# A two-layer hybrid backbone on one core: where the modulation bias is added

## The chip, the cores and the metric

The kernel runs on one core of a Trainium2 chip. Its time is the device time of one execution in microseconds (us), as the median of several runs. A trace of one execution shows every instruction of the five engines (PE is TensorE, with PEld its weight loads; DVE is VectorE; ACT is ScalarE; POOL is GpSimd; SP issues most of the loads) and the DMA queues.

## The reference

Two layers (weights differ per layer) run over 256 latent tokens and 256 context tokens of width 1024. All is float32. Before its mixers and before its FFN, each layer normalises the tokens and modulates them with a shift and a scale; each of the two residual branches is multiplied by a gate. These six vectors per layer come from one matrix-vector product with a bias, once for the latents (input `c`) and once for the context (input `c_ctx`):

```
s_c, s_cc = silu(c), silu(c_ctx)
m_l = split(s_c  @ w_mod[l] + b_mod[l], 6)     # latents: shift, scale, gate, shift, scale, gate
m_c = split(s_cc @ w_mod[l] + b_mod[l], 6)     # context
p   = (rms_norm(x) * (1 + m[1]) + m[0]) @ w_in[l]
x   = x + m[2] * merge(S5(p), retention(p), GLA(p), gates(p)) @ w_out[l]
x   = x + m[5] * swiglu(rms_norm(x) * (1 + m[4]) + m[3])
```

`w_mod[l]` is 1024 x 6144 and `b_mod[l]` 6144 long. The rest is three token mixers (a complex diagonal scan, retention, gated linear attention), three merge projections, an output projection and an FFN of width 2816. The change touches only how `+ b_mod[l]` is done.

## The kernel before, in words

**Weights.** Large products are made of three float32r products: each weight tile of 512 KB is loaded by SP into one of 3 `raw` buffers, split into a high part on ACT (line 264) and a low part on DVE (line 265) into one of 4 `hi`/`lo` pairs, and multiplied on PE (lines 243, 247 to 249). Weight loads and splits are traced with a priority 20000 instructions ahead of their place (`W_AHEAD`).

**The modulation vectors.** `self.sil` holds silu of both inputs, 128 rows by 8 blocks by 32 columns, of which two columns are in use (context, latent). The product of a vector is cut into four quarters of 256 columns. Quarter q is a product of 128 rows by 32 columns, written to partitions 32q to 32q+31 of one PSUM bank; rows 32q and 32q+1 are the context's and the latents' result.

- `mod_vec(l, m, gds)` (lines 340 to 396) makes ten of the twelve vectors, one at a time, beside the layers' own work: a list of "asides" is advanced by one step wherever the main code calls `tick()` (line 419). It loads a row of `b_mod` (line 347), begins the PSUM accumulation with four products of one row (`self.one`, all ones, times a quarter of the bias row; lines 348 to 350), loads eight blocks of `w_mod` of 512 KB into the two `wm` buffers (line 357), and adds their products. For the six vectors in `ON_VECTOR` the eight blocks are instead multiplied and summed on DVE (lines 362 to 367) and brought into PSUM at the end by products with `self.unit` (lines 369 to 372). Then ACT copies the bank into `rows` (line 376). Gates go to DRAM by four small stores (line 380); shifts and scales are transposed on PE and spread over `self.mod` by DVE (lines 383 to 395).
- `mod_chunk(c, brow)` (lines 431 to 459) makes the first two vectors of layer 0 in four chunks of 256 columns each at the start of the kernel. Both bias rows lie in the two `wm` buffers until the last chunk has used them (lines 1324 to 1327). Each chunk starts with four one-row products of 128 columns (line 445); ACT copies the result (line 451), PE transposes it, DVE spreads it (lines 455 to 458), `norm_chunk` modulates the tokens with it, and `pack_mms` multiplies them with the first weights.

**Order.** Each engine and each DMA queue works its instructions in order. The order is made by a planner that runs the program through its own timing model: an engine that is free takes the ready instruction of highest priority; an instruction whose buffer is not free is not ready. Tiles of the two arenas (`arena`, `zone`) are places chosen by the program, and a write waits for the last use of its place. SP's queue holds nearly all the loads, ACT's the token loads at the start, POOL's the small parameters.

Of the kernel before, what the change touches and what calls it, by code (L numbers as in the profile page):

```python
# [10 lines left out]
F32 = mybir.dt.float32  # L11
F32R = mybir.dt.float32r
U8 = mybir.dt.uint8
AF = mybir.ActivationFunctionType
ALU = mybir.AluOpType
# [4 lines left out]
D = 1024  # L20
KD = 8
# [118 lines left out]
class Hybrid:  # L140
# [199 lines left out]
    def mod_vec(self, l, m, gds):  # L340
        nc, i = self.nc, self.i
        b = self.bank(self.sd)[:, :256]
        ring = lambda: self.wmod.tile([128, D], F32, tag="wm", name=self.nm("wm"))
        c0 = D * m
        with self.prio(-W_AHEAD - self.delta):
            brow = self.new(D)
            self.q["mod"].dma_start(out=brow.ap[0:1], in_=i["b_mod"][l:l + 1, c0:c0 + D])
        for q in range(4):
            self.mm_(b[32 * q:32 * q + 32], self.one[0:1], brow.ap[0:1, 256 * q:256 * q + 256], True, False,
                     tile_position=(0, 32 * q))  # L350
        dve = (l, m) in ON_VECTOR
        who = (1,) if l and m > 1 else (0, 1)
        acc = {x: self.new(D) for x in who} if dve else {}
        for k in range(KD):
            with self.prio(-W_AHEAD - self.delta):
                w = ring()
                self.q["mod"].dma_start(out=w, in_=i["w_mod"][l, 128 * k:128 * k + 128, c0:c0 + D])
            if not dve:
                for q in range(4):
                    self.mm_(b[32 * q:32 * q + 32], self.sil[:, k], w[:, 256 * q:256 * q + 256], False, k == KD - 1,  # L360
                             tile_position=(0, 32 * q))
            for x, a in acc.items():
                c = self.sil[:, k, x:x + 1]
                if k:
                    self.stt(a.ap, w, c, a.ap, ALU.mult, ALU.add)
                else:
                    self.ts(a.ap, w, c, None, ALU.mult)
            yield
        for x, a in acc.items():
            for q in range(4):  # L370
                self.mm_(b[32 * q:32 * q + 32], self.unit[:, x], a.ap[:, 256 * q:256 * q + 256], False, x == 1,
                         tile_position=(0, 32 * q))
            self.drop(a)
        self.drop(brow)
        rows = self.new(256)
        self.act(rows.ap, b, AF.Copy)
        if m in (2, 5):
            gd = gds[m]
            for q in range(4):
                self.q["gd"].dma_start(out=gd[:, 256 * q:256 * q + 256], in_=rows.ap[32 * q:32 * q + 2])  # L380
            self.drop(rows)
            return
        tb = self.bank(self.sd)
        for k in range(2):
            self.transpose(tb[:, 128 * k:128 * k + 128], rows.ap[:, 128 * k:128 * k + 128])
        tv = tb[:, :256].rearrange("p (k q s) -> p q k s", q=4, s=32)[:, :, :, 0:2]
        idx = {0: 0, 1: 1, 3: 2, 4: 3}[m]
        dst = self.mod[:, l, idx].rearrange("p (q k) s -> p q k s", k=2)
        if m in (1, 4):
            g0 = 32 * l + (0 if m == 1 else 8)  # L390
            for s in range(2):
                self.stt(dst[:, :, :, s], tv[:, :, :, s], 1.0,
                         self.par[:, g0:g0 + 8].rearrange("p (q k) -> p q k", k=2), ALU.add, ALU.mult)
        else:
            nc.vector.tensor_copy(dst, tv)
        self.drop(rows)
# [34 lines left out]
    def mod_chunk(self, c, brow):  # L431
        nc, i = self.nc, self.i
        b = self.bank()
        ws = {}
        for m in (1, 0):
            ws[m] = (self.zone if c == 3 and m else self.arena).new(KD, 256)
            self.q["modc"].dma_start(out=ws[m].ap, in_=i["w_mod"][0][:, D * m + 256 * c:D * m + 256 * c + 256].rearrange(
                "(k p) c -> p k c", p=128))
        for k in range(KD + 1):
            for q in range(4):  # L440
                m, hf = q // 2, q % 2
                o = b[32 * q:32 * q + 32, :128]
                if k == 0:
                    c0 = 256 * c + 128 * hf
                    self.mm_(o, self.one[0:1], brow[m][0:1, c0:c0 + 128], True, False, tile_position=(0, 32 * q))
                else:
                    self.mm_(o, self.sil[:, k - 1], ws[m].ap[:, k - 1, 128 * hf:128 * hf + 128], False, k == KD,
                             tile_position=(0, 32 * q))
        self.drop(*ws.values())
        rows = self.new(128)  # L450
        self.act(rows.ap, b[:, :128], AF.Copy)
        tb = self.bank()
        self.transpose(tb[:, :128], rows.ap)
        tv = tb[:, :128].rearrange("p (m k s) -> p m k s", m=2, s=32)
        for s in range(2):
            self.stt(self.mod[:, 0, 1, 2 * c:2 * c + 2, s], tv[:, 1, :, s], 1.0, self.par[:, 2 * c:2 * c + 2],
                     ALU.add, ALU.mult)
        nc.vector.tensor_copy(self.mod[:, 0, 0, 2 * c:2 * c + 2], tv[:, 0, :, 0:2])
        self.drop(rows)
# [855 lines left out]
    def layer(self, l):  # L1315
        nc = self.nc
# [4 lines left out]
        if l == 0:  # L1321
            with self.prio(-2 * W_AHEAD):
                self.load_params()
                brow = [self.wmod.tile([128, D], F32, tag="wm", name=self.nm("wm")) for _ in range(2)]
                xin = [self.x_in(t) for t in range(4)]
                for m in range(2):
                    self.q["par0"].dma_start(out=brow[m][0:1], in_=self.i["b_mod"][0:1, D * m:D * m + D])
                xs = [self.xscale(x.ap, self.arena if t > 1 else self.zone) for t, x in enumerate(xin)]
                hold = self.zone.new(1536)
                self.drop(*xin)  # L1330
                banks = [self.bank(self.mm) for _ in range(4)]
                for c in range(4):
                    self.mod_chunk(c, brow)
                    self.norm_chunk(c, xs)
                    self.pack_mms(banks, self.pack_weights(0, 0, c), c)
                self.drop(*xs)
            gqk = self.pack_out(0, banks, u_dr)
            self.load_params2()
        else:
            self.need("mod10")  # L1340
            gqk = self.pack_early(l, u_dr)
            self.drop(*self.xt[:2])
            x_dr = self.dram.tile([2, 128, D], F32, name=self.nm("xdr"))
            for t in range(2):
                self.q["xst"].dma_start(out=x_dr[t], in_=self.xt[2 + t].ap)
                self.drop(self.xt[2 + t])
# [107 lines left out]
```

## Time and profile before

| | |
|---|---|
| timed runs (3) | 1404.64, 1400.70, 1400.59 us; median 1400.7 |
| profiled execution, first to last instruction | span 1395.2 us (mean granted TensorE clock 0.985) |
| what lies around the span | 5.5 us, median less span |
| busy: PE / PEld / DVE / ACT / POOL | 1344.3 / 1140.9 / 908.3 / 577.4 / 75.6 us |
| instructions | 22070 |

The profiled execution's own device time is not given; its span and the 5.5 us around it are what the numbers below are added to. Busy time of an engine says little by itself; PE is busy 96% of the span, and where it is busy without a pause a product that goes can shorten the run. A chain of waits, followed back from the end, says which work set the end.

### The profile page before, as it was taken

The page shows a single profiled execution, that of the slowest core. Times are in us where ns is not written, and L with a number is a line of the kernel's source. Part 1 is how long each engine was busy: PE and PEld are TensorE (multiplying, and loading weights), DVE is VectorE, ACT ScalarE, POOL GpSimd, SP SyncE. Part 2 cuts the span into 40 slices and gives each one's busy share as a digit, 9 for nine tenths or more (in the row PEclk, how much of TensorE's full clock was granted, in tenths as well). Part 3 has the DMA queues.
Part 4 walks back from the last instruction along what each step waited for, and adds up shares of the span by engine and source line. Part 5 has one row for each costly group of instructions (what it writes and reads, how often), then busy time and mean ns, then how long its engine had stood idle before and what let it go on. Part 6 is the DMA issues. An engine that isn't in the chain of part 4 may idle for free.

```text
span 1395.2 us, 22070 instructions
## 1 busy us (share of the span) xinstructions
PE 1344.3 (96%) x8559; PEld 1140.9 (82%) x8559; DVE 908.3 (65%) x1423; ACT 577.4 (41%) x930; POOL 75.6 (5%) x111
## 2 busy tenths in 40 slices
PE   4899999999999999999999999999999999899996
PEld 3788888787777778788777778888999997899985
DVE  4579782838889564545554788645876778555555
ACT  3367352323432343222222447545564364444442
POOL 3310000001100020000000000100000100000000
PEclk9999999999999999999999999999999999899999
DMA  9744465668968554733344786644766866466662
GB/s 305 213 115 119 139 200 182 213 197 271 303 210 280 173 165 125 234 109 121 106 129 129 279 310 193 181 112 111 199 170 163 238 191 215 117 198 197 184 192 91
DMA packets 258817, 257.33 MB, mean 184 GB/s; under 512 B 27200, under 2 KB 219244, under 8 KB 258200
## 3 DMA queue, kind: packets, MB, share of 16 engines
q1 hardware_dynamic: 244360, 230.41, 55.0%
q10 hardware_dynamic: 11392, 20.39, 4.2%
q0 software_dynamic: 2960, 5.12, 1.4%
q8 instruction: 67, 1.10, 0.3%
q14 instruction: 38, 0.31, 0.1%
HBM read 231.79 MB, written 24.08 MB: 183 GB/s over the span
## 4 chain that ended last, share of the span: by engine, by line
PE 85%; DMA 6%; DVE 5%; issue 2%; ACT 2%; SPq 1%; DVEq 0%; POOL 0%; POOLq 0%; ACTq 0%
PE b L243 83%; PE b L253 2%; DVE arena L231 2%; DVE lo L231 1%; DMA wm<-in_w_mod_dram 1%; DMA arena<-in_w_mod_dram 1%; DMA raw<-in_w_in_dram 1%; DMA raw<-in_w_ffn_out_dram 1%; DMA arena<-wb 1%; ACT arena L228 1%; DMA arena<-in_ctx_dram 1%; ACT hi L228 1%; DVE rb L231 0%; DVE zone L234 0%; DMA raw<-in_w_ffn_in_dram 0%
## 5 line engine op out<-in xcount | busy, mean ns | idle before, releaser
L243 PE MATMUL b<-rb,hi 128*128 128x256 f32 (+1 forms) x2784 | 695.1, 340 | 6.2 <-ACT rb L228 4.7
L243 PEld LDWEIGHTS b<-rb,hi 128*128 128x128 f32 x2784 | 481.9, 193 | 70.1 <-issue 11.1
L228 ACT ACTIVATE hi<-raw 128x1024 fp32r<-128x1024 f32 (+3 forms) x298 | 293.0, 989 | 458.0 <-PE b L243 350.4
L243 PE MATMUL b<-rb,lo 128*128 128x256 f32 (+1 forms) x1392 | 471.3, 339 | 0.0
L231 DVE TENSOR_TENSOR lo<-raw,hi 128x1024 fp32r<-128x1024 f32 (+3 forms) x298 | 338.3, 1140 | 199.4 <-ACT hi L228 190.4
L243 PE MATMUL b<-hi,rb 128*128 128x512 f32 (+2 forms) x1168 | 346.2, 374 | 3.9 <-DVE arena L570 3.3
L243 PEld LDWEIGHTS b<-rb,lo 128*128 128x128 f32 x1392 | 268.7, 193 | 31.7 <-issue 5.4
L243 PEld LDWEIGHTS b<-hi,rb 128*128 128x128 f32 x1168 | 216.5, 188 | 39.2 <-issue 4.1
L243 PE MATMUL b<-lo,rb 128*128 128x512 f32 (+2 forms) x584 | 217.0, 373 | 0.0
L243 PE MATMUL b<-arena 64*64 64x96 f32 (+8 forms) x1104 | 132.8, 288 | 0.3 <-DVE arena L231 0.3
L243 PEld LDWEIGHTS b<-lo,rb 128*128 128x128 f32 x584 | 109.8, 188 | 15.3 <-issue 1.3
L243 PEld LDWEIGHTS b<-arena 128*128 128x128 f32 (+4 forms) x1104 | 102.6, 167 | 20.2 <-issue 7.1
L231 DVE TENSOR_TENSOR arena<-arena 128x512 f32<-128x512 f32 (+5 forms) x174 | 105.6, 622 | 17.7 <-ACT arena L228 16.7
L234 DVE SCALAR_TENSOR_TENSOR arena<-arena,b 128x512 f32<-128x512 f32 (+1 forms) x136 | 74.2, 552 | 51.0 <-PE b L243 50.6
L228 ACT ACTIVATE arena<-b 128x512 f32<-128x512 f32 (+6 forms) x138 | 66.5, 486 | 73.9 <-PE b L243 59.6
L228 ACT ACTIVATE rb<-arena 128x256 fp32r<-128x256 f32 (+3 forms) x133 | 60.8, 473 | 84.3 <-PE b L243 57.2
L231 DVE TENSOR_TENSOR zone<-zone 128x512 f32<-128x512 f32 (+6 forms) x127 | 73.7, 604 | 28.6 <-DMA wb<-zone 17.4
L234 DVE SCALAR_TENSOR_TENSOR zone<-wm,sil,zone 128x1024 f32<-128x1024 f32 x56 | 70.9, 1283 | 18.7 <-DMA wm<-in_w_mod_dram 18.3
L231 DVE TENSOR_TENSOR rb<-arena,rb 128x256 fp32r<-128x256 f32 (+2 forms) x106 | 54.4, 522 | 21.1 <-ACT rb L228 20.7
L228 ACT ACTIVATE arena<-arena 128x512 f32<-128x512 f32 (+3 forms) x61 | 36.5, 601 | 30.6 <-DVE arena L231 19.9
L253 PE MATMUL b<-cst,arena 128*128 128x128 f32 (+1 forms) x178 | 30.4, 290 | 18.8 <-DMA arena<-in_norm_mix_dram 9.6
L491 POOL TENSOR_TENSOR st<-st,mh 128x1 f32<-128x1 f32 x16 | 11.6, 727 | 658.9 <-DVE st L240 657.9
(137 smaller groups left out, 660.4 us busy)
## 6 DMA issues: line engine op xcount, KB each, us to landing
raw<-in_w_ffn_in_dram SPq DMA_DIRECT2D x88, 512.0 KB
wm<-in_w_mod_dram SPq DMA_DIRECT2D x80, 512.0 KB
raw<-in_w_ffn_out_dram SPq DMA_DIRECT2D x66, 512.0 KB
raw<-in_w_in_dram SPq DMA_DIRECT2D x48, 512.0 KB
raw<-in_w_in_dram SPq DMA_DIRECT2D x48, 384.0 KB
raw<-in_w_out_dram SPq DMA_DIRECT2D x16, 512.0 KB
arena<-in_w_mod_dram SPq DMA_DIRECT2D x7, 1024.0 KB
wb<-zone ACTq DMA_DIRECT2D x8, 512.0 KB
```

The costliest lines, as they stand in the source:

```text
L228: self.S.activation(out, in_, f, bias=bias, scale=scale)
L231: self.V.tensor_tensor(out=out, in0=a, in1=b, op=op)
L234: self.V.scalar_tensor_tensor(out=out, in0=a, scalar=s, in1=b, op0=op0, op1=op1)
L243: self.P.matmul(out, l, r, start=start, stop=stop, **k)
L253: self.P.transpose(out, in_, self.ident[:k, :k])
L491: self.G.tensor_tensor(out=st[:, 3:4], in0=st[:, 2:3], in1=self.mh[:, 0:1], op=ALU.pow)
```

## The change

The one-row products go. The bias is loaded to the partitions where the result lies (32q and 32q+1, both rows the same), over a buffer that POOL has set to zero, and DVE adds it while it copies the result out of PSUM, where ACT copied it before. The first product of each accumulation now opens it. In `mod_vec` the bias buffer is 256 columns instead of 1024 and becomes the result; its one load becomes four. At the start the two `wm` buffers with bias rows become one, zeroed by POOL, and the two loads become four.

```diff
@@ mod_vec
         with self.prio(-W_AHEAD - self.delta):
-            brow = self.new(D)
-            self.q["mod"].dma_start(out=brow.ap[0:1], in_=i["b_mod"][l:l + 1, c0:c0 + D])
-        for q in range(4):
-            self.mm_(b[32 * q:32 * q + 32], self.one[0:1], brow.ap[0:1, 256 * q:256 * q + 256], True, False,
-                     tile_position=(0, 32 * q))
+            brow = self.new(256)
+            nc.gpsimd.memset(brow.ap, 0.0)
+            for q in range(4):
+                self.q["mod"].dma_start(out=brow.ap[32 * q:32 * q + 2],
+                                        in_=i["b_mod"][l, c0 + 256 * q:c0 + 256 * q + 256].partition_broadcast(2))
...
-                    self.mm_(b[32 * q:32 * q + 32], self.sil[:, k], w[:, 256 * q:256 * q + 256], False, k == KD - 1,
+                    self.mm_(b[32 * q:32 * q + 32], self.sil[:, k], w[:, 256 * q:256 * q + 256], k == 0, k == KD - 1,
...
-                self.mm_(b[32 * q:32 * q + 32], self.unit[:, x], a.ap[:, 256 * q:256 * q + 256], False, x == 1,
+                self.mm_(b[32 * q:32 * q + 32], self.unit[:, x], a.ap[:, 256 * q:256 * q + 256], x == who[0], x == 1,
...
-        self.drop(brow)
-        rows = self.new(256)
-        self.act(rows.ap, b, AF.Copy)
+        rows = brow
+        self.tt(rows.ap, b, brow.ap, ALU.add)
@@ mod_chunk
-        for k in range(KD + 1):
+        for k in range(KD):
...
-                if k == 0:
-                    c0 = 256 * c + 128 * hf
-                    self.mm_(o, self.one[0:1], brow[m][0:1, c0:c0 + 128], True, False, tile_position=(0, 32 * q))
-                else:
-                    self.mm_(o, self.sil[:, k - 1], ws[m].ap[:, k - 1, 128 * hf:128 * hf + 128], False, k == KD,
-                             tile_position=(0, 32 * q))
+                self.mm_(b[32 * q:32 * q + 32, :128], self.sil[:, k], ws[m].ap[:, k, 128 * hf:128 * hf + 128], k == 0,
+                         k == KD - 1, tile_position=(0, 32 * q))
...
-        self.act(rows.ap, b[:, :128], AF.Copy)
+        self.tt(rows.ap, b[:, :128], brow[:, c], ALU.add)
@@ layer, at the start of layer 0
-                brow = [self.wmod.tile([128, D], F32, tag="wm", name=self.nm("wm")) for _ in range(2)]
+                brow = self.wmod.tile([128, D], F32, tag="wm", name=self.nm("wm"))[:, :512]
+                nc.gpsimd.memset(brow, 0.0)
+                brow = brow.rearrange("p (c j) -> p c j", j=128)
                 xin = [self.x_in(t) for t in range(4)]
-                for m in range(2):
-                    self.q["par0"].dma_start(out=brow[m][0:1], in_=self.i["b_mod"][0:1, D * m:D * m + D])
+                for q in range(4):
+                    self.q["par0"].dma_start(out=brow[32 * q:32 * q + 2], in_=self.i["b_mod"][
+                        0, D * (q // 2):D * (q // 2) + D].rearrange("(c h j) -> h c j", h=2, j=128)[q % 2].partition_broadcast(2))
```

## Rows read from the trace of the kernel before

**Rows 1.** The page: busy time of each engine; the chain of waits by engine.

```profile
PE 1344.3 (96%) x8559; PEld 1140.9 (82%) x8559; DVE 908.3 (65%) x1423; ACT 577.4 (41%) x930; POOL 75.6 (5%) x111
PE 85%; DMA 6%; DVE 5%; issue 2%; ACT 2%; SPq 1%; DVEq 0%; POOL 0%; POOLq 0%; ACTq 0%
```

**Rows 2.** Stretches: length; PE, PEld, DVE, ACT, POOL busy; clock; DMA share; GB/s.

```profile
10.00:11.00 1.00, 0.05 (x1) 0.00 (x0) 0.36 (x3) 0.19 (x2) 0.31 (x1) 1.00 0.98 384
48.00:50.00 2.00, 1.64 (x61) 1.37 (x52) 2.00 (x4) 0.78 (x2) 1.51 (x3) 1.00 0.96 254
450.00:650.00 200.00, 199.99 (x1067) 160.15 (x1066) 105.80 (x149) 63.23 (x101) 8.51 (x12) 1.00 0.51 155
776.00:838.00 62.00, 61.68 (x305) 48.16 (x303) 50.40 (x62) 30.49 (x46) 0.00 (x0) 1.00 0.88 312
```

**Rows 3.** Groups of PE, shapes apart: the one-row products of `mod_vec`.

```profile
L243 PE MATMUL b<-zone,one 1*32 1x256 f32 x80 | 6.3, 386 | 1.3 <-DMA zone<-in_b_mod_dram 1.3
```

**Rows 4.** Timeline of PE, three places: start, time, line, operation, count, idle before.

```profile
244.55 0.63 PE L243 MATMUL b<-zone,one 1*32 1x256 f32 x8
245.12 1.07 PE L243 MATMUL b<-wm,sil 128*32 128x256 f32 x16
...
389.02 0.62 PE L243 MATMUL b<-rb,hi 128*128 128x512 f32 x2
389.48 0.39 PE L243 MATMUL b<-rb,lo 128*128 128x512 f32 x1
389.79 0.63 PE L243 MATMUL b<-zone,one 1*32 1x256 f32 x8
390.36 0.73 PE L243 MATMUL b<-rb,hi 128*128 128x512 f32 x2
390.93 0.39 PE L243 MATMUL b<-rb,lo 128*128 128x512 f32 x1
...
410.33 0.63 PE L243 MATMUL b<-zone,one 1*32 1x256 f32 x8 [1.34 <-DMA zone<-in_b_mod_dram]
```

**Rows 5.** The chain that ended last, in order of time, two stretches: start, time.

```profile
289.73 8.69 DMA arena<-wb
...
321.61 8.50 PE b L243 x57
...
754.58 21.85 PE b L243 x119
...
838.30 13.25 PE b L243 x57
```

**Rows 6.** Groups of DVE by shape: sums of two tensors that are near.

```profile
L231 DVE TENSOR_TENSOR arena<-b,arena 128x256 f32<-128x256 f32 x8 | 3.4, 422 | 0.4 <-PE b L243 0.3
L231 DVE TENSOR_TENSOR rb<-raw,rb 128x128 fp32r<-128x128 f32 x8 | 2.3, 291 | 4.4 <-ACT rb L228 4.3
```

**Rows 7.** Timeline of the first 48 us, three engines: PE, DVE, SP.

```profile
46.18 0.33 PE L253 MATMUL b<-cst,arena 128*128 128x128 f32 x1 [1.40 <-ACT arena L228]
...
45.69 1.29 DVE L231 TENSOR_TENSOR lo<-raw,hi 128x768 fp32r<-128x768 f32 x2 [6.76 <-ACT hi L228]
...
47.94 1.00 SPq L357 DMA_DIRECT2D wm<-in_w_mod_dram  x2
```

**Rows 8.** SP's waits up to 60 us: us in total, times, longest.

```profile
SPq L1327 <- DMA arena<-in_ctx_dram: 3.1, 1, 3.1
SPq L437 <- DMA arena<-in_ctx_dram: 2.2, 1, 2.2
```

**Rows 9.** Bias loads of `mod_vec` (min/median/max ns) and two in SP's timeline.

```profile
L347 SPq DMA_DIRECT2D zone<-in_b_mod_dram x10: 243/258/288, 222.1 to 800.5; - x10
222.12 5.09 SPq L347 DMA_DIRECT2D zone<-in_b_mod_dram x2
```

**Rows 10.** Timeline of POOL: a memset; a load that waited.

```profile
39.08 0.52 POOL L760 MEMSET arena<- 128x512 f32 x1 [0.98 <-PE b L243]
447.44 1.72 POOL L991 DMA_DIRECT2D zone<-in_s_b_re_dram  x2 [91.32 <-DMA gd<-zone]
```

More of the change, by code (lines that the diff above doesn't have):

```diff
@@ L438, in mod_chunk @@
                 "(k p) c -> p k c", p=128))
-        for k in range(KD + 1):
+        for k in range(KD):
             for q in range(4):
                 m, hf = q // 2, q % 2
-                o = b[32 * q:32 * q + 32, :128]
-                if k == 0:
-                    c0 = 256 * c + 128 * hf
-                    self.mm_(o, self.one[0:1], brow[m][0:1, c0:c0 + 128], True, False, tile_position=(0, 32 * q))
-                else:
-                    self.mm_(o, self.sil[:, k - 1], ws[m].ap[:, k - 1, 128 * hf:128 * hf + 128], False, k == KD,
-                             tile_position=(0, 32 * q))
+                self.mm_(b[32 * q:32 * q + 32, :128], self.sil[:, k], ws[m].ap[:, k, 128 * hf:128 * hf + 128], k == 0,
+                         k == KD - 1, tile_position=(0, 32 * q))
         self.drop(*ws.values())
         rows = self.new(128)
-        self.act(rows.ap, b[:, :128], AF.Copy)
+        self.tt(rows.ap, b[:, :128], brow[:, c], ALU.add)
         tb = self.bank()
```

## The prediction

> **What bounds the kernel now.** I read the page first: PE is busy 96% of the span and holds 85% of the chain that ended last; DVE is next with 65% [rows 1]. Then the stretches, since a share is a mean. From 450 to 650 us PE pauses for 0.01 us in 200: there a product that goes shortens the run by its slot. In 776:838 PE is as full, but DVE is busy 81% and the DMA engines 88% at 312 GB/s; in 48:50, at the start, DVE is busy all the time [rows 2]. Third the chain in order of time, to see which of two full engines sets the pace. It leaves PE twice in the range of the change: from 289.73 us (DRAM round trips and scans of the S5 mixer) until 321.61, and from 776.43 (754.58 + 21.85) until 838.30, where it runs through loads of `w_mod` and FFN weights, high parts on ACT, low parts and `mod_vec` sums on DVE [rows 5]. What PE saves inside these two stretches is slack; before and between them it counts.
>
> **The change part by part.**
>
> *One-row products of `mod_vec`: removed.* Ten vectors by four products are 40, seen as 80 records, 6.3 us busy, and PE waited 1.3 us for one bias row [rows 3]. What a site costs is read from starts [rows 4]. Where the vector's own products follow at once, 245.12 - 244.55 = 0.57 us; four sites do (244, 291, 445, 506 us). Where it stands alone between 512-column products, these run at (389.48 - 389.02) / 2 = 0.23 us; from 389.48 to 390.93 there are three of them and the site, so 1.45 - 0.69 = 0.76 us: the products around it lose 0.2 us as well. Six sites are so (338, 390, 410, 577, 784, 810 us); that at 410.33 has the wait of 1.34 us besides. In all 4 x 0.57 + 6 x 0.76 + 1.34 = 8.2 us leave PE's queue. Of these, the sites at 291 (0.57), 784 and 810 (2 x 0.76) lie in the two stretches where the chain is not PE's, and count nothing. That leaves 6.1 us. The wait at 410: PE has no other pause near it, so what comes late next can only be DVE, which I give nothing there; if it is as late, 1.3 us less.
>
> *The sum on DVE: added; ACT's copy: removed.* Ten DVE sums of 128x256 with one operand in PSUM. The same form elsewhere takes 0.422 us [rows 6]. Eight lie in stretches where PE sets the pace and DVE has over a third of its time free: nothing. The two of the last vectors (near 799 and 826 us) are in line on DVE where the chain runs through it: 2 x 0.42 = 0.84 us, with 0 below if their wait for a load hides them. ACT is idle enough that its copies give nothing back. Behind each sum wait the low parts queued on DVE, which PE needs only some tiles later (four `hi`/`lo` pairs).
>
> *Bias loads.* Four for one: 30 more issues on SP, 0.258 us each [rows 9], 7.7 us over 1400, hidden by the three `raw` buffers; in 776:838 at most one vector's three more, 0.8 us, which I leave to the range. They are needed only at the end of a vector, so their landing is hidden. POOL's ten memsets are half of a 128x512 one of 0.52 us [rows 10], on an engine busy 5%: nothing.
>
> *The start.* Four chunks lose four one-row products each. Those of the first two chunks ran while PE waited for `w_mod` anyway, those of the fourth between waits: nothing; the third's, in a full stretch of PE, half a 256-column site, 0.3 us. The result now passes DVE: a 128x128 sum is 0.29 us [rows 6]. For the first two chunks DVE is free. For the last two it lies in 44:54, where DVE is full: 2 x 0.29 = +0.6 us. Here is the widest unknown, the third chunk's order on DVE. Before, PE's transposes waited 1.40 us at 46.18 because ACT split a weight ahead of its copy; if DVE now takes the sum ahead of its low parts (45.69 to 46.98), that goes: -1.4. If behind them, the sum ends at 46.98 + 0.29 instead of before 46.18: +1.1 [rows 7]. Each is as likely; I take the 0.6 and 0.3 between. Next, one `wm` buffer is free from the start. Its first 512 KB were loaded at 47.94, as soon as the bias rows were used, though needed at 245 [rows 7, 4]: the planner takes a load when its buffer is free. It will now stand among the first loads, 512 KB at 384 GB/s [rows 2] or 1.4 us; it counts if it delays the fourth chunk's weights (which ended in the split at 45.69) and these are then what is waited for: 0 to +1.4, and I take 0.4, since the chunk's products are 10 us later. Last, SP: the first bias load and a `w_mod` load waited for the context tokens, which they don't use (3.1 and 2.2 us) [rows 8]; the eighth load before each is what fits, four of SP and four of ACT being ahead of the first. Two more bias loads push the first `w_mod` loads two turns back, behind the second context block and the first of `x`. The DMA engines are then full with those tokens (98% in 10:11, 384 GB/s) [rows 2], so little is lost: 0 to +2.8, and I take 0. Start in all: +0.6 - 0.3 + 0.4 = +0.7 us, between -1.7 (-1.4 - 0.3) and +5.6 (1.1 + 0.6 + 1.4 + 2.8 - 0.3).
>
> *Sum.* -6.1 + 0.8 + 0.7 = -4.6 us on a span of 1395.2; with the 5.5 us around it, the median of 1400.7 becomes 1396.1. With each unknown at its end, from 1400.7 - 8.2 - 1.7 = 1390.8 (all sites count, DVE's sums hidden, a good start) to 1400.7 - 6.1 + 1.3 + 0.8 + 0.8 + 5.6 = 1403.1.
>
> **The rivals.**
>
> *All of it counts.* The chain's leaving PE need not mean that PE has slack: at 838.30 PE paused little, and 61.68 of 62 us in 776:838 it was busy [rows 2]. If DVE is late there only because the planner lets it be, all 8.2 us count, DVE's sums cost nothing, and the third chunk gains 1.4 + 0.3: 1390.8. Against it: 88% DMA share there.
>
> *The start gives most of it back.* The extra `w_mod` load goes ahead of the fourth chunk's weights (+1.4), the sum of the third stands behind their low parts (+1.1), the first `w_mod` pair is 2.2 us late (the second's wait of before). With 0.6 for the full DVE and the 0.3 saved that is +5.0 against -6.1 + 0.8: 1400.4, no change. For it: the DMA engines are full at the start, 98% in 10:11 [rows 2]. Against: three things must meet.
>
> *Slower: the bias loads hold SP's queue.* One mechanism: a bias load waits for POOL's memset and for the eighth load before it, and all weight loads stand behind it. Its place is where the chain goes through loads: the start and 776:838. Two bias loads in a row once took 5.09 us [rows 9]; a vector now has four in a row. If each of the two vectors in 776:838 holds the queue for those 5.1 us, and the start loses 2.8, that is +13.0 against -6.1 + 0.8 + 0.7: 1409.1. It decides from where the hold is longer than the buffers cover; below 2.3 us a vector it stays a gain. For it: POOL's head once waited 91 us for a store [rows 10], and a memset behind such a head would hold SP too. Against: bias loads were issued far ahead of their use, all but one. The Trainium skill, "DMA: Bandwidth & Descriptors", section "Rules for kernel authors", speaks for it: "Many small transfers | Coalesce into one large transfer; under 64 KB you're paying mostly overhead". The change splits 4 KB in four. By the 2.0 us of fixed cost in its section "Anatomy of one DMA", fitted there to POOL's loads, 30 more are an estimated 60 us if none of it were hidden; the trace shows 0.26 us of SP each and one wait of PE.
>
> That the products would not go is no rival: nothing else of the kernel issues them.
>
> **How the numbers follow.** The sum above: 0.43. All of it counts: 0.20. The start gives it back: 0.24. SP's queue held: 0.13. The median is 1396.1, the likeliest's own range 1392 to 1400. The range for 8 in 10 goes from 1390 (the second case) to 1404 (past the third, into part of the fourth). A measurement of this kernel tells about 0.3%, 4.2 us: faster is below 1396.5, slower above 1404.9. Faster holds the second case and a little over half of the first with some of the third's better half: 0.49; no change the rest of the first and most of the third: 0.37; slower the fourth: 0.14.
>
> **What would show it.** In the trace after: no `one` products on PE, and 512-column products running on at 0.23 us where sites stood; at 410 no pause; ten DVE sums of 0.42 us reading PSUM and `zone`; PE full in 450:650. For the start: where the sum of the third chunk stands to the low parts at 45, when the first `w_mod` load is issued, and whether PE's pause of 1.40 at 46 us is gone. For the held queue: SP waiting at line 347's successors with weights late behind, and pauses of PE after 776. The prediction is wrong if PE's busy time falls by less than 6 us, or if it falls and the pauses grow by as much elsewhere than at the start.

## The result, and the profile after

The changed kernel takes 1418.3 us (median of 5 runs, 1412.4 to 1420.3) against 1400.7: the ratio is 1.0118, 95% interval 1.0096 to 1.0140. It is slower by 17.6 us, where 4.6 us less was forecast. Its page has these lines (span; busy time; the chain that ended last, by engine):

```profile
span 1416.3 us, 21921 instructions
PE 1347.5 (95%) x8447; PEld 1144.1 (81%) x8447; DVE 916.3 (65%) x1437; ACT 571.8 (40%) x916; POOL 78.9 (6%) x122
PE 78%; DMA 9%; issue 4%; DVE 4%; ACT 2%; SPq 2%; POOL 0%; ACTq 0%; DVEq 0%; POOLq 0%
```

PE has 112 products fewer (records of the trace) and is busy 3.2 us longer than in [rows 1]; PE's share of the chain fell from 85% to 78%. Stretches of the kernel before and of the changed one show where (length; PE, PEld, DVE, ACT, POOL busy; granted clock; DMA share; GB/s). First the kernel before:

```profile
0.00:110.00 110.00, 85.39 (x632) 70.71 (x633) 67.75 (x160) 48.23 (x83) 30.74 (x59) 0.98 0.69 205
110.00:440.00 330.00, 328.35 (x2159) 264.96 (x2158) 245.98 (x369) 128.76 (x200) 16.11 (x14) 0.99 0.68 209
440.00:900.00 460.00, 459.37 (x2419) 365.48 (x2418) 277.04 (x380) 165.88 (x264) 12.06 (x17) 1.00 0.56 178
900.00:1395.00 495.00, 471.24 (x3356) 439.74 (x3353) 317.55 (x517) 234.52 (x383) 16.72 (x21) 0.97 0.59 170
```

Then the changed kernel, with the two stretches that answer to [rows 2] at the end:

```profile
0.00:110.00 110.00, 81.86 (x577) 67.62 (x578) 67.27 (x165) 44.68 (x76) 32.15 (x62) 0.95 0.69 205
110.00:440.00 330.00, 319.82 (x2070) 256.86 (x2068) 237.44 (x355) 126.33 (x195) 24.77 (x30) 0.96 0.67 204
440.00:900.00 460.00, 456.75 (x2364) 366.41 (x2364) 282.49 (x385) 159.39 (x250) 5.61 (x9) 1.00 0.55 173
900.00:1416.00 516.00, 489.11 (x3441) 453.24 (x3439) 329.08 (x534) 241.43 (x398) 16.40 (x21) 0.97 0.59 170
...
450.00:650.00 200.00, 199.11 (x1048) 160.01 (x1047) 111.69 (x159) 60.95 (x95) 3.21 (x4) 1.00 0.51 160
776.00:838.00 62.00, 59.63 (x265) 47.33 (x264) 42.22 (x51) 23.46 (x34) 0.00 (x0) 0.97 0.76 253
```

The reader is to take two numbers from each: the pause (length less PE's busy time) and the loss to the clock (length times what is missing of 1.00). In 110:440 PE's pauses grew from 1.7 to 10.2 us and the loss to the clock from 1.7 to 13.7 (from stretches of 1 us; the rounded clocks above give 3.3 and 13.2). Over the whole span the pauses are 68.8 us instead of 50.9 (+17.9), and the loss to the clock is 35.4 instead of 20.9 (span times one less the mean clock of 0.975 and 0.985). Part of this loss lies in the pauses. Taken in slices of 1 us, the loss inside PE's busy time is 26.3 us instead of 15.0 (+11.3), and PE's work at the full clock is 1321.2 instead of 1329.3 (-8.1). The three differences sum to the +21.1 of the spans. So the work did leave PE, 8 us of it, and 29 us of pauses and half-speed came in its place. A second profile of the kernel before (c_before below) has 57.2, 11.7 and 1331.2 us: single profiles differ by some us.

**What came as foreseen.** No product with `one` is left. The ten sums on DVE take 0.42 us, the 40 bias loads 0.25 us of SP each, and no product waits for a bias load (groups of DVE; the loads with min/median/max ns):

```profile
L231 DVE TENSOR_TENSOR zone<-b,zone 128x256 f32<-128x256 f32 x10 | 4.2, 417 | 2.6 <-PE b L243 2.6
...
L349 SPq DMA_DIRECT2D zone<-in_b_mod_dram x40: 231/252/446, 218.0 to 754.7; - x40
```

**The start.** The timelines that answer to [rows 7], SP, PE and DVE (start, time, what, idle before):

```profile
5.09 3.24 SPq L1323 DMA_DIRECT2D wm<-in_b_mod_dram  x4
8.38 2.06 SPq L436 DMA_DIRECT2D arena<-in_w_mod_dram  x2
...
33.18 3.05 SPq L357 DMA_DIRECT2D wm<-in_w_mod_dram  x1
...
39.26 0.33 PE L253 MATMUL b<-cst,arena 128*128 128x128 f32 x1 [1.67 <-DVE arena L231]
43.53 0.30 PE L243 MATMUL b<-arena,sil 128*32 128x128 f32 x2 [2.14 <-DMA arena<-in_w_mod_dram]
57.17 0.33 PE L253 MATMUL b<-cst,arena 128*128 128x128 f32 x1 [0.41 <-DVE arena L231]
62.22 1.28 PE L243 MATMUL b<-rb,hi 128*128 128x512 f32 x4 [3.14 <-ACT rb L228]
...
56.83 0.29 DVE L231 TENSOR_TENSOR arena<-b,wm 128x128 f32<-128x128 f32 x1 [5.43 <-PE b L243]
```

The first `w_mod` pair is issued at 8.38 us, two turns later, and the first `wm` load at 33.18, as worked out. But the planner made another order of it: the third chunk comes sooner (its transposes at 39.26 instead of 46.18, behind a pause of 1.67 us where 1.40 stood), and the fourth's products run in four pieces among the third's, until 56.8 us, so that its row is summed at 56.83. Before, ACT copied it at 49.71:

```profile
49.71 0.28 ACT L228 ACTIVATE arena<-b 128x128 f32<-128x128 f32 x1 [1.21 <-PE b L243]
```

PE then pauses 3.14 us, and its clock is at half level (1.2 GHz) from 63.2 for 6.8 us.

**Near 420 us.** The chain in order of time (start, time, what):

```profile
396.08 4.29 DMA wm<-in_w_mod_dram
400.37 0.02 issue
400.40 1.02 DVE zone L238
401.42 0.03 issue
401.45 6.94 DMA wm<-in_w_mod_dram
...
409.80 4.88 DMA wm<-in_w_mod_dram
...
418.75 5.20 DMA wm<-in_w_mod_dram
...
425.25 1.30 DVE rb L231 x2
426.55 0.04 issue
426.59 5.67 PE b L243 x18
```

DVE works in order; the sums of a vector on DVE stand ahead of the low part that PE needs, and each waits for its 512 KB of `w_mod`, of which only two fit. PE pauses 9.29 us before 426.59, and its granted clock is 0.53 in 421:432. DVE's operations on `wm` show this wait over the kernel (us, times), first before, then the changed kernel:

```profile
  DMA wm<-in_w_mod_dram: 22.2, 17
...
  DMA wm<-in_w_mod_dram: 42.8, 29
```

Beside these loads POOL's of the second layer's S5 preparation run now, which waited until 447 us before [rows 10]:

```profile
399.55 0.31 POOL L347 MEMSET zone<- 128x256 f32 x1 [25.94 <-PE b L243]
400.07 1.77 POOL L985 DMA_DIRECT2D zone<-in_s_b_re_dram  x2 [0.20 <-issue]
```

**Where the loss is made.** Both kernels have 5928 products of a token block with a weight part. Counted by these (the n-th of one against the n-th of the other, where the two orders agree), the changed kernel is 7 us late where before stands at 65 us, 13 at 193, 12 at 403 and 20 at 420; from 450 us on it stays 18 to 23 us late. So the whole loss is made in the first 440 us.

### The profile page after: what moved, and what is told of

It reads as the page before. It is cut to its first block, busy times and chain, and to the rows that moved or that the text cites. A ratio compares the mean times of both kernels' runs of the same rounds, so it can differ in the third digit from the quotient of the medians.

```text
span 1416.3 us, 21921 instructions
## 1 busy us (share of the span) xinstructions
PE 1347.5 (95%) x8447; PEld 1144.1 (81%) x8447; DVE 916.3 (65%) x1437; ACT 571.8 (40%) x916; POOL 78.9 (6%) x122
## 4 chain that ended last, share of the span: by engine, by line
PE 78%; DMA 9%; issue 4%; DVE 4%; ACT 2%; SPq 2%; POOL 0%; ACTq 0%; DVEq 0%; POOLq 0%
PE b L243 77%; DMA wm<-in_w_mod_dram 5%; PE b L253 1%; DVE zone L234 1%; DMA arena<-in_w_mod_dram 1%; ACT arena L228 1%; DVE lo L231 1%; SPq L436 1%; DVE arena L231 1%; DMA arena<-in_x_dram 1%; ACT hi L228 1%; SPq L534 0%; DMA udr<-arena 0%; DMA arena<-gdr 0%; DMA zone<-in_s_log_dt_dram 0%
## 5 line engine op out<-in xcount | busy, mean ns | idle before, releaser
L243 PEld LDWEIGHTS b<-lo,rb 128*128 128x128 f32 x584 | 110.6, 189 | 17.9 <-DVE lo L231 2.6
L243 PEld LDWEIGHTS b<-arena 128*128 128x128 f32 (+4 forms) x1104 | 104.9, 170 | 19.3 <-issue 6.7
L228 ACT ACTIVATE arena<-b 128x512 f32<-128x512 f32 (+4 forms) x134 | 65.5, 493 | 80.8 <-PE b L243 63.8
L231 DVE TENSOR_TENSOR rb<-arena,rb 128x256 fp32r<-128x256 f32 (+2 forms) x106 | 54.6, 523 | 26.4 <-ACT rb L228 26.2
L228 ACT ACTIVATE arena<-arena 128x512 f32<-128x512 f32 (+3 forms) x61 | 36.6, 599 | 32.6 <-DVE arena L231 15.2
L228 ACT ACTIVATE zone<-b 128x512 f32<-128x512 f32 (+3 forms) x44 | 17.5, 397 | 63.3 <-PE b L243 33.1
```

The source lines that it names most:

```text
L228: self.S.activation(out, in_, f, bias=bias, scale=scale)
L231: self.V.tensor_tensor(out=out, in0=a, in1=b, op=op)
L243: self.P.matmul(out, l, r, start=start, stop=stop, **k)
```

## The experiments

Each was timed against the kernel before on the same chip (median there 1398.3 to 1402.8). Each run also gives its span and mean granted clock. Their product is an estimate of the span at the full clock; the rest of the span is the loss to half level (in pauses too). The kernel before has a product of 1376.4 to 1377.6 us and a loss of 21.7 to 23.8 (medians); its single runs keep the product within 1372 to 1383 while the loss goes from 15 to 34, so this division is sharper than the time.

| kernel | ratio to before (95%) | time us | at full clock us | loss us |
|---|---|---|---|---|
| changed kernel | 1.0118 (1.0096 to 1.0140) | 1418.3 | 1380.8 | 35.4 |
| e1_vec_only: vectors only | 0.9996 (0.9972 to 1.0020) | 1402.7 | 1375.5 | 25.2 |
| e2_start_only: start only | 1.0128 (1.0071 to 1.0186) | 1420.1 | 1385.9 | 32.6 |
| e3_wide: all, old buffer size | 1.0027 (0.9990 to 1.0064) | 1406.0 | 1372.5 | 30.9 |
| e5_no_products: before less 40 products | 0.9980 (0.9957 to 1.0002) | 1399.1 | 1372.5 | 25.1 |
| e4_hold_wm: all, no early load | 1.0101 (1.0032 to 1.0169) | 1415.2 | 1382.8 | 31.1 |
| e7_start_act: start, rows on ACT | 1.0051 (1.0024 to 1.0077) | 1408.3 | 1380.3 | 26.0 |
| e8_hoist_only: before, early load | 1.0084 (1.0052 to 1.0115) | 1413.1 | 1381.7 | 29.6 |
| c_before: before again | 0.9996 (0.9966 to 1.0027) | 1400.8 | 1376.3 | 23.1 |
| e9_act_hold: start, both undone | 1.0068 (1.0047 to 1.0090) | 1410.5 | 1381.9 | 25.4 |
| e12_start_dvecopy: before, rows on DVE | 1.0136 (1.0092 to 1.0179) | 1419.2 | 1380.5 | 36.9 |
| e13_prep_last: all, preparation last | 1.0118 (1.0077 to 1.0158) | 1418.8 | 1381.5 | 35.4 |
| e11_vec_wide: vectors only, old buffer size | 0.9934 (0.9904 to 0.9965) | 1390.8 | 1366.2 | 23.6 |
| e14_start_no_products: before less 12 products | 0.9987 (0.9961 to 1.0014) | 1401.0 | 1375.5 | 23.1 |
| e15_wide_mc2000: all, old size, chunks and their loads raised | 1.0086 (1.0056 to 1.0115) | 1414.8 | 1386.2 | 25.4 |
| e6_dve_copy: before, vectors' rows on DVE | 0.9962 (0.9938 to 0.9987) | 1397.2 | 1375.0 | 20.9 |
| e11_again | 0.9919 (0.9888 to 0.9949) | 1392.9 | 1364.7 | 26.4 |
| e16_wide_chunk: all, old size, chunk raised | 1.0009 (0.9972 to 1.0046) | 1403.2 | 1372.0 | 29.4 |
| e17_chunk: all, chunk raised | 1.0131 (1.0077 to 1.0184) | 1419.7 | 1381.3 | 35.4 |

**The two halves of the change.** e1 takes the diff's `mod_vec` alone, e2 all the rest alone.

> Only `mod_vec` is changed; the start is that of before. Theory A (the start gives 7 us away by the order of its chunks, `mod_vec` the rest): 1400.7 + 9 = about 1410, with the pause of 9 us of PE near 420 still there and the first 150 large products where they were before (75 us). Theory B (the loss near 420 and the clock's dips follow from the start's new order alone): at or below 1397.

> Only the start is changed; `mod_vec` is that of before. Theory A: the 150th large product comes 7 us later, no pause near 420: about 1408. Theory B: all of the loss, about 1416. Theory C (each plan that differs falls out by some us either way): anything from 1395 to 1415, and the parts don't add up.

The start carries the whole loss: 1.0128, +18 us. The vectors alone gain nothing.

**The bias buffer's size.** e3 is the changed kernel with

```diff
-            brow = self.new(256)
+            wide = self.new(D)
+            brow = Obj(wide.arena, wide.off, wide.n, wide.ap[:, :256])
```

> The changed kernel, but each vector's bias buffer takes 1024 columns of `zone` as before, of which 256 are used. Theory A (the 768 columns set free let the second layer's S5 loads on POOL run at 400 us instead of 447 us, among the `w_mod` loads that DVE waits for): the pause near 420 goes, about 1409. Rival (DVE's sums and POOL's memsets make the pause, not the place): about 1418, pause still there.

That gives back most of the loss. The same lines with the start of before are e11, later run again:

> The changed vectors with the start of before, and bias buffers of the old size (1024 columns of the zone, of which 256 are used). If the start carries the loss and the small buffers the rest, it is the best of both: some 4 to 7 us less than before at full clock (span times granted clock near 1371 to 1373), 1394 to 1399 in time. If the buffer's size did nothing by itself: as the changed vectors alone, 1400 to 1404.

> The best version once more, in five rounds: changed vectors, start of before, bias buffers of the old size. Expected is the ratio of before, 0.990 to 0.997, so 1388 to 1396; a ratio over 0.998 would say that the first result was chance.

It is the fastest of all, 9 to 11 us under before, and at the full clock 10 to 13 us under. Between e1 and e11 stands only the size of a buffer of which 256 columns are used: 10 us. PE's pauses in all are 58.5 us in e1 and 50.4 in e11 (52.8 when run again; span less busy time). In 110:440 they are 4.5 us in e1 and 2.1 in e11:

```profile
110.00:440.00 330.00, 327.93 (x2117) 265.60 (x2116) 245.07 (x371) 127.72 (x196) 26.99 (x30) 0.98 0.68 209
```

DVE's waits for `w_mod` parts (us, times) and one kind of the preparation's loads (first and last start at the end) show what else differs. First e1, then e11:

```profile
  DMA wm<-in_w_mod_dram: 36.5, 24
...
L990 POOL DMA_DIRECT2D zone<-in_s_b_re_dram x4: 830/840/849, 99.8 to 408.0; - x4
```

```profile
  DMA wm<-in_w_mod_dram: 29.8, 20
...
L991 POOL DMA_DIRECT2D zone<-in_s_b_re_dram x4: 829/836/842, 98.5 to 283.4; - x4
```

With the old size the second layer's preparation loads at 283 us, with the small one at 408, among the vectors' loads.

**The products alone.** e5 leaves the 40 products out and their load, buffer and copy in.

> The kernel before with the forty one-row products of the ten vectors left out (so their bias is missing in the result); bias load, its buffer and ACT's copy stay. If PE's slots count where the chain is PE's, as in the prediction: 1400.7 - 6.1 = about 1394.6, between 1392.5 and 1396. Theory C (the planner's new order outweighs the slots): off by some us, with clock dips or pauses at new places.

At the full clock it is 4.5 us under before, the time 2.8 us with an interval that ends at no change: the loss to the clock took the rest back.

**Parts of the start.** e4 keeps the second `wm` buffer in use until the fourth chunk; e7 lets ACT copy the rows in e2 (their bias is left out; one column on POOL per chunk keeps the bias buffer in use); e8 puts one bias row of before in `zone`, whose space is then taken earlier; c_before is the kernel before:

```diff
# e4, added to the changed kernel
+                self.held = self.wmod.tile([128, D], F32, tag="wm", name=self.nm("wm"))[:, :1]
+                nc.gpsimd.memset(self.held, 0.0)
...
+        if c == 3:
+            self.G.tensor_tensor(out=self.held, in0=self.held, in1=rows.ap[:, 0:1], op=ALU.add)
# e7, in the start alone
-        self.tt(rows.ap, b[:, :128], brow[:, c], ALU.add)
+        self.act(rows.ap, b[:, :128], AF.Copy)
...
# e8, in the kernel before (hold moved up)
-                brow = [self.wmod.tile([128, D], F32, tag="wm", name=self.nm("wm")) for _ in range(2)]
+                brow = [self.wmod.tile([128, D], F32, tag="wm", name=self.nm("wm")), hold.ap[:, :D]]
```

> The changed kernel, but the second wm buffer is held until the fourth chunk's rows are done (a memset of one column and one column's sum on POOL), so that no wm load can go ahead of the fourth chunk's weights. Theory 1 (the freed buffer: the early 512 KB load delays the fourth chunk, and the order planned behind it is the one that loses): the start's +7.4 us of PE shrinks to under 2, and the time falls from 1418 to about 1400 to 1405. Theory 2 (the sum on DVE instead of the copy on ACT reorders the start): nothing changes, 1416 to 1420. Theory 3 (no single part: any shifted order meets longer pauses and more half-clock stretches): somewhere between, 1404 to 1414.

> The changed start alone (vectors 2 to 11 as before), but a chunk's rows are copied out by ACT as before instead of summed on DVE; the bias of the first two vectors is left out, and one column on POOL keeps the bias buffer in use until the fourth chunk. The wm load is still early. Theory 1 (early load): as the changed start alone, 1416 to 1422. Theory 2 (sum on DVE): back to 1400 to 1404. Theory 3 (no single part): 1405 to 1415.

> The kernel before, with its bias products and ACT copies, but the second of the start's two bias rows lies in the zone space that is held there anyway, so that one wm buffer is free from the start and its 512 KB load goes between the two loads of the fourth chunk. Theory 1 (early load): slower by about as much as the changed start alone, 1412 to 1420. Theory 2 (sum on DVE) and theory 3 in its weak form: 1399 to 1404.

> The kernel before once more, with a second profile: what a measurement tells of no change (ratio 1.000 within 0.003), and whether the half-clock stretches of its first profile (26, 412, 914, 1061, 1115, 1187 and 1388 us) are the program's or the execution's. If they are the program's they stand at the same places; if the execution's, those in full stretches of PE come and go by some 3 to 10 us in all, while those behind a pause stay.

None fits one theory. Without the early load the changed kernel loses 1.0%; the early load alone, with `zone`'s space taken earlier, costs 0.8%; with ACT's copies back, 0.5% is left. The second profile of before has its late half-level stretches (after 900 us) at nearly the same places, but those at 26 and 412 us are gone and one stands at 109: single early stretches belong to the execution.

Then both suspects undone, and one alone in the kernel before:

```diff
# e12, in the kernel before
-        self.act(rows.ap, b[:, :128], AF.Copy)
+        nc.vector.tensor_copy(rows.ap, b[:, :128])
```

> The changed start alone with both suspects undone: rows copied out by ACT, and the second wm buffer held until the fourth chunk is done; the four bias loads, the memset and the missing one-row products of the start stay (the first two vectors' bias is left out). If the two suspects make up the start's loss (theory 1 and 2 together), it is back at the kernel before: 1399 to 1404, and span times granted clock near 1377. If the loss comes with any order other than that of before (theory 3), it stays at 1405 to 1415.

> The kernel before with one edit: the four chunks' rows are copied out of PSUM by DVE instead of ACT. Bias products, loads and buffers are as before, so no wm load is early. Theory 2 (DVE in the fourth chunk's line is the start's cost): PE's pauses of the first 110 us grow by 2 to 4 us, with a pause near 59 us, and the time is 1406 to 1416. Theory 1 (early load): 1400 to 1403.

e12 is the clearest run: four copies of 128x128 on DVE instead of ACT, nothing else, and a loss as large as the whole is there, +19 us. It is made up otherwise: 4 us at the full clock and 15 of half level, where e2 has 9 and 10. DVE copies the fourth row at 59.22, behind four pieces of its products again, and PE pauses 3.29 us before 64.58. Its first two stretches:

```profile
0.00:110.00 110.00, 84.25 (x607) 67.88 (x608) 67.82 (x167) 44.65 (x77) 32.59 (x63) 0.95 0.71 210
110.00:440.00 330.00, 323.01 (x2066) 259.79 (x2065) 224.38 (x332) 122.34 (x193) 10.38 (x10) 0.94 0.63 192
```

In 110:440 the clock costs it 19 us, the pauses 7. But e9 stays at 1.0068 with both undone, so they are not all: left in it are the four bias loads, the memset, the missing products and small operations on POOL that keep the buffers in use. e14 asks whether any other order is worse, with a removal:

```diff
# e14, in the kernel before
-                    self.mm_(o, self.one[0:1], brow[m][0:1, c0:c0 + 128], True, False, tile_position=(0, 32 * q))
+                    if c == 3:
+                        self.mm_(o, self.one[0:1], brow[m][0:1, c0:c0 + 128], True, False, tile_position=(0, 32 * q))
...
```

> The kernel before without the one-row products of the first three chunks (12 products; their part of the first two vectors' bias is left out); loads, buffers, ACT copies and the fourth chunk stay. Less work on PE and nothing more anywhere. If each edit of the start costs by itself (load, buffer, engine), this one costs nothing: 1398 to 1402, span times granted clock 1376 to 1378. If any other order of layer 0 is worse than that of before, a pure removal is slower too: 1405 to 1414.

Nothing is lost. But the question stays open, for e14 has no other order: its large products (a token block with a weight part) come in the order of before from first to last, and up to 400 us within 2.5 us of it. The traces divide the kernels without exception. Where the order of these products leaves that of before within the first 90 us (all kernels with the changed start or a part of it, e8 and e12), the time is longer than that of the same vectors with the start of before; where it is kept up to 460 us or longer (e1, e5, e6, e11, e14), it is not. So in the start the edits that moved a result, a load or a buffer each cost by themselves, and they don't add up. That before has an order that happens to suit it, so that nearly any other start loses, is a rival that no run here tests.

**The split fourth chunk.** e15 raises `mod_chunk` and its loads by 2000 in priority, e16 and e17 only its products, sum and spread, by 300:

```diff
# e16 (old buffer size) and e17 (as changed)
+        with self.prio(-300):
             for k in range(KD):
...
```

> The changed kernel with bias buffers of the old size, and the four chunks' loads, GEMV, rows and transposes emitted ahead of the norm and the products of the chunks before them in priority. If the cost of the DVE rows is that the fourth chunk's rows come 7 us later (56.8 instead of 49.7 us) and PE pauses for it near 59, this takes it away: 1393 to 1400, with no pause over 2 us between 55 and 65. If the order behind the start is what costs, it stays at 1403 to 1412.

> The changed kernel with bias buffers of the old size, and the chunks' products, row sum and spread (not their loads) 300 higher in priority, so that the fourth chunk's products stay together instead of in three pieces between the third's. If the split chunk and its late row (sum at 56.8 us) are the start's cost, PE's pause of 3.1 us near 59 to 62 goes, the first 110 us return to within 2 us of before, and the time is 1391 to 1398, as with the start of before. If the cost lies in the order behind the start, 1403 to 1412, as without the edit.

> The changed kernel with the same raise of the chunks' products, row sum and spread, and its small bias buffers. If the split chunk is the start's cost: as the changed vectors alone, 1400 to 1406. If not: 1414 to 1420, as the changed kernel.

e15 says nothing of it: the chunks' loads went ahead of the constants, and the first product came at 27.36 us. In e16 and e17 the fourth chunk is in one piece, yet a pause of 2.7 us stands at 60 us, now behind the S5 tables on DVE, and the first 110 us hold 27.5 and 27.4 us of pauses (24.6 before). e17 is as slow as the changed kernel. So keeping the chunk in one piece does not give the loss back. The pair shows the buffer's size once more: in e17 POOL's preparation loads run at 400.94 and PE pauses 8 us at 418; in e16 the last of them of this kind started at 285.7, and there is no pause there.

**The pause at 420.** e13 lists the second layer's S5 preparation last among the asides.

> The changed kernel with the second layer's S5 preparation put last in the order of the side work, so that its loads (12 on POOL, at 400 to 406 us in the changed kernel, just when the vectors' w_mod parts are waited for) come later. Theory A (these loads make the w_mod parts late): PE's pause of 9.3 us at 417 falls to 4 or less, with the half-clock stretch behind it, and the time to 1406 to 1411. Theory B (the pause is from DVE's order, vector sums ahead of the low parts): the pause stays over 7 us and the time 1415 to 1420.

The pause fell from 9.3 to 5.2 us, between the two theories, and the time stayed: another pause ends at 645.7 us, where the preparation was then late:

```profile
PE b L253 <- DVE zone L231: 8.3, 1, 8.3
...
PE b L243 <- DVE zone L234: 5.2, 1, 5.2
```

A pause of about 4 us stands there without these loads too. In e7 and e9, whose vectors are those of before, the preparation's loads start at 446 and 447 us, and PE pauses all the same:

```profile
417.59 0.50 PE L243 MATMUL b<-rb,hi 128*128 128x512 f32 x1 [4.12 <-DVE rb L231]
...
419.29 0.80 PE L243 MATMUL b<-rb,hi 128*128 128x512 f32 x1 [3.91 <-DVE rb L231]
```

**The vectors' sums on DVE.** e6 is the kernel before with `nc.vector.tensor_copy(rows.ap, b)` in place of ACT's copy of a vector.

> The kernel before with one edit: the ten vectors' rows are copied out of PSUM by DVE instead of ACT (0.42 us each); products, bias loads and buffers stay. By the prediction's step (eight hidden, two in line) it is 0.8 us slower: 1400 to 1403. If ten more instructions in DVE's line make the low parts late, span times granted clock grows by 3 us or more and the time is over 1405.

Faster by 0.4%, where 0.8 us more was forecast. In its one profile PE's pauses in 110:440 are gone, and the clock is full:

```profile
110.00:440.00 330.00, 329.97 (x2179) 265.29 (x2178) 249.03 (x377) 129.15 (x198) 15.48 (x14) 1.00 0.68 213
```

## Why the prediction was wrong

**The step that failed is the start: "+0.7 us, between -1.7 and +5.6".** The start alone costs 18 us (e2). Its facts were foreseen: the four bias loads (3.24 us), the `w_mod` pair two turns later (PE's pauses up to the first chunk's products are 17.5 instead of 17.3 us in all, up to the second's 20.1 instead of 19.3, so 0 was near as a direct price), the early 512 KB. Wrong was the way to price them. I shifted single rows in the order of before, asked only where the third chunk's sum would stand to its low parts (-1.4 or +1.1), and took a mean. The planner makes the whole order anew: the third chunk came 7 us sooner and the fourth's row 7 us later, and the third chunk's sum stood ahead of the low parts (38.92 against 47.24), yet the pause that this was to take away is there (1.67 us). Moving the rows alone is enough (e12, 1.0136). In all kernels with the chunks' rows on DVE the 150th product of a token block with a weight part starts 3 to 8 us later than the 74.7 us of before (16 in e15), in all with rows on ACT 1.2 us sooner to 1.0 later. That delay is not the only way to lose: e8, where it starts sooner, is 12 us slower.

**No term was there for the clock.** I counted PE's slots at one speed. Of the 17.6 us, some 13 are loss to half level (35.4 against 22.4 us, medians of all runs), some 4 are time at the full clock. Half-level stretches follow PE's long pauses (63, 422 us), but some stand in full stretches: in 158:169 PE is busy throughout at 0.53, where before ran at 1.00. My sign that "PE's busy time falls by less than 6 us" would refute the forecast came true, by these stretches.

**The bias buffer's size had no term.** I priced the four loads, the memset and the issue, and not the 768 columns of `zone` that come free. They cost about what the products gain: e1 at 1402.7, e11 at 1390.8. In the changed kernel and in e17 POOL's preparation loads then run at 400 us, beside the vectors' loads, and PE pauses 8 to 9 us; with the old size and the changed vectors they have run before 290 us (e3, e11, e16), and the pause is 4.0, 1.7 and none. So the buffer's size moves these loads, and not later but sooner when it is large. In e1, with the small buffer and the start of before, they run at 407 and the pause is 4.5. That these loads lengthen the pause fits e13, whose order differs in more than these loads, but the pause can be only part of the 10 us: PE's pauses in 110:440 differ by 2.4 us between e1 and e11. Through which waits the rest comes is not shown.

**The products: "6.1 us count" had the right size, and may be high.** What leaves PE is of the size foreseen: 8.1 us of work at the full clock with the start's products, where the prediction had 8.2 with a wait of 1.34 us. Removed alone, the 40 products give 4.5 us at the full clock and 2.8 in time (e5). With the sums on DVE it is 10 to 13 at the full clock (e11), more than the products can give, so the order has a part in it. That sites at 291, 784 and 810 count nothing was neither shown nor refuted.

**The sums on DVE: "+0.84", "ACT is idle enough that its copies give nothing back".** Sign wrong: e6 gains 0.4%. Whether a copy was in ACT's way, or the new order is better by chance, I have not shown.

**The rivals.** "The start gives most of it back" (1400.4) had the place and a quarter of the size. The slower one, SP's queue held by bias loads, came nearest in time (1409.1), by luck, for its mechanism was wrong: 40 loads at 0.25 us, and with SP's first four at 5.09 to 8.33 PE's first product with `w_mod` starts at 17.95, where before had 18.51. The 5.09 us that priced it were not the loads' own: SP waited 4.5 us for PE between the two. Nor does its bound of 2.3 us a vector count the 2.8 us that it gave to the start. The rule that it drew on, in the Trainium skill, "DMA: Bandwidth & Descriptors", section "Rules for kernel authors", against many small transfers, did not decide: no wait of PE for a bias load is left in the trace, where before had two, of 1.37 and 1.34 us. "All of it counts" (1390.8) is what the vectors' half does when its buffer keeps its size.

In sum, from the runs: about -10 us for the vectors' arithmetic (e11), +10 for the small buffer (e1 against e11), +18 for the start (e2): +18, and 17.6 was measured. So close a sum is luck: with the old buffer size the changed start costs 13 to 15 us (e3 against e11), and with the changed start the small buffer costs 12 (changed kernel against e3). What stays open is why e9, with rows on ACT and no early load, still loses 0.7%, why a new order of the start loses at all, and through which steps of layer 0 it does.

## What to carry to other kernels

In a program that a planner orders, an operation that changes its engine, a load that can go sooner or a buffer that shrinks is a new order, not a cost of its own: time each part of such a change alone, for its good part (here 0.992) may hide behind a bad one. Multiply each run's span by its granted clock before reading a time; pauses and half-level loss tell more than busy shares. Keep the size and place of buffers while the arithmetic changes, and shrink them in a second step.

## What the runs showed of the hardware

The clock fell to half where PE had no pause: in the changed kernel its last one before the fall near 158 us is 0.49 us long, at 114. What PE does around the fall is 44 products of 96 columns from 154.88 us and 16 of 64 rows by 112 columns from 160.18; groups of the same two kinds ran at 1.00 in the kernel before. First the changed kernel, then before:

```profile
158.00:169.00 11.00, 11.00 (x53) 8.02 (x49) 6.85 (x11) 3.52 (x7) 0.00 (x0) 0.53 0.05 10
```

```profile
158.00:169.00 11.00, 11.00 (x96) 9.01 (x95) 6.33 (x10) 2.58 (x6) 0.00 (x0) 1.00 0.31 101
```

What makes it fall in one and not in the other no run here shows. It is no mark of a slow kernel: in e11, the fastest, the granted clock is 0.57 in 167:175, with PE busy throughout. And of two 512 KB loads of one queue near 400 us one took 4.3 us and the next 6.9, at a DMA share of 0.79 in 395:400 and 0.83 to 1.07 in 400:410.
